# Routing weights loaded in one transfer behind the first input tile, and put in order by block transposes

## The chip, the cores and the metric

The kernel runs on one core of one Trainium2 chip. The metric is the device time of one execution in microseconds (us). A core has several engines with a queue of instructions each; those that matter here are VectorE (DVE), ScalarE (ACT) and SyncE (SP, which only issues transfers). All transfers between the main memory (HBM) and the on-chip memory (SBUF, 128 partitions) are carried by 16 DMA engines.

## The reference

```python
def setup_inputs():
    batch, seq, hidden, n_experts = 16, 1024, 512, 8
    k = 2
    ...

def reference(x, expert_indices, expert_weights):
    batch, seq, hidden = x.shape
    k = expert_indices.shape[-1]
    x_expanded = x[:, :, np.newaxis, :].repeat(k, axis=2)
    weights = expert_weights[..., np.newaxis]
    return (x_expanded * weights).astype(np.float32)
```

There are 16 x 1024 = 16,384 tokens. Each token's row of 512 float32 numbers is written out twice, once multiplied by each of its two weights. `expert_indices` is not used. The input x is 33.6 MB, the output 67.1 MB, the weights 128 KB.

## The kernel before

The 16,384 tokens are cut into 8 tiles of 2,048 tokens. In a tile, partition p holds 16 consecutive tokens (`TX = 16`): 16 rows of 512 numbers, 32 KB that lie in one piece in HBM. An x tile is therefore one transfer of 128 pieces of 32 KB (4 MB), an output tile one of 8 MB, 64 KB per partition in two halves of 8 tokens.

The weights of all tiles lie in one SBUF tile `w_tile` of 128 partitions x 256 numbers: 32 columns per token tile (16 tokens times 2). Partition p of tile g needs the 32 numbers of its own 16 tokens, a piece of 128 bytes in HBM. Line 57 loads them by 8 transfers on SP's queue, one for each token tile, each of 128 pieces of 128 bytes (16 KB). They are the first things in SP's queue.

`load(i)` (line 71) takes one of two x buffers and issues the transfer of x tile i on ScalarE's queue (line 78). Two tiles are loaded ahead; `load(i + 2)` stands at the end of the loop body for tile i.

The loop (line 83) runs over the 8 tiles. For each of the 16 tokens of a partition there are two multiplies of 128x512 numbers by a column of `w_tile`: VectorE makes copy 0 (`tensor_scalar`, line 99), ScalarE copy 1 (`mul`, line 93). Output tiles have two buffers. When the 16th token is done, SP issues the transfer of the output tile (line 109); the first tile alone is written in two halves, the first of them after 8 tokens. The output transfers stand in SP's queue behind the 8 weight transfers.

The waits between engines are put in by the framework, from what each instruction reads and writes. In the built program the first multiply of each engine waits for the first weight transfer and for the first x tile. Completions of transfers are counted on 8 semaphores taken in turn, so that some transfers wait for an earlier one that used the same semaphore: in this program the second x transfer waits for the second weight transfer, the eighth weight transfer for the first x tile, and the first output halves for the third and fifth weight transfer. The load of ScalarE's function table stands in ScalarE's queue behind the first two x transfers.

Of the kernel before, what the change touches and what calls it, by code (L numbers as in the profile page):

```python
# [1 line left out]

# [4 lines left out]


@with_exitstack
def kernel(  # L10
    ctx: ExitStack,
    tc: tile.TileContext,
    x: bass.AP,
    expert_indices: bass.AP,
    expert_weights: bass.AP,
    out: bass.AP,
):
    nc = tc.nc

    batch, seq, hidden = x.shape  # L20
    k = expert_weights.shape[-1]
    P = nc.NUM_PARTITIONS
    ntok = batch * seq
    assert ntok % P == 0
    A_TOTAL = ntok // P

    f32 = mybir.dt.float32
    row = k * hidden
    TX = 16
    TO = 16  # L30
    HALF = TO // 2
    PAD = 8


    groups = [[16], [16], [16], [16], [16], [16], [16], [16]]
    assert sum(sum(g) for g in groups) == A_TOTAL

    xf = x.rearrange("b s h -> (b s) h")
    of = out.rearrange("b s k h -> (b s) (k h)")
    wf = expert_weights.rearrange("b s k -> (b s) k")  # L40

    w_pool = ctx.enter_context(tc.tile_pool(name="w_pool", bufs=1))
    x_pool = ctx.enter_context(tc.tile_pool(name="x_pool", bufs=2))
    o_pool = ctx.enter_context(tc.tile_pool(name="o_pool", bufs=2))

    w_tile = w_pool.tile([P, A_TOTAL * k], f32)

    def rows(of_all, done, T):
        return of_all[done * P : (done + T) * P, :].rearrange(
            "(p a) n -> p (a n)", a=T  # L50
        )

    weights = []
    for group in groups:
        weights.append((sum(n for _, n in weights), sum(group)))
    for at, T in weights:
        nc.sync.dma_start(out=w_tile[:, at * k : (at + T) * k], in_=rows(wf, at, T))  # L57

    tiles = []
    done = 0  # L60
    for group in groups:
        T = sum(group)
        a0 = 0
        for n in group:
            tiles.append((done, T, a0, n))
            a0 += n
        done += T

    loaded = []

    def load(i):
        if i >= len(tiles):
            return
        done, T, a0, n = tiles[i]
        x_tile = x_pool.tile([P, TX * hidden], f32)
        cols = rows(xf, done, T)[:, a0 * hidden : (a0 + n) * hidden]
        for lo, hi in [(0, P)]:
            nc.scalar.dma_start(out=x_tile[lo:hi, : n * hidden], in_=cols[lo:hi, :])
        loaded.append(x_tile)

    for i in range(2):
        load(i)
    for i, (done, T, a0, n) in enumerate(tiles):
        x_tile = loaded[i]
        outr = rows(of, done, T)
        for t in range(n):
            if t % TO == 0:
                o_tile = o_pool.tile([P, 2, HALF * row + PAD], f32)
            for kk in range(k):
                c = (done + a0 + t) * k + kk  # L90
                h, o = t // HALF, t % HALF * row + kk * hidden
                if kk == 1:
                    nc.scalar.mul(  # L93
                        out=o_tile[:, h, o : o + hidden],
                        in_=x_tile[:, t * hidden : (t + 1) * hidden],
                        mul=w_tile[:, c : c + 1],
                    )
                    continue
                nc.vector.tensor_scalar(  # L99
                    out=o_tile[:, h, o : o + hidden],  # L100
                    in0=x_tile[:, t * hidden : (t + 1) * hidden],
                    scalar1=w_tile[:, c : c + 1],
                    scalar2=None,
                    op0=mybir.AluOpType.mult,
                )

            if t + 1 == TO or (i == 0 and t + 1 == HALF):
                halves = slice(h if i == 0 else 0, h + 1)
                nc.sync.dma_start(  # L109
                    out=outr.rearrange("p (b n) -> p b n", b=2)[:, halves, :],  # L110
                    in_=o_tile[:, halves, : HALF * row],
                )
        load(i + 2)

# [1 line left out]
_INS = ['x', 'expert_indices', 'expert_weights']  # L116
_OUTS = [((16, 1024, 2, 512), 'float32')]


# [23 lines left out]
```

## Time and profile before

| what | value |
|---|---|
| time, median of 4 runs | 240.77 us (239.89 to 241.2) |
| the profiled execution: its own time | 240.8 us |
| the profiled execution: its span | 239.0 us |
| busy: VectorE, ScalarE | 51.4 us (22%), 80.7 us (34%) |
| moved by the DMA engines | 100.81 MB in 4498 packets, mean 422 GB/s |
| queue q1 (SP's): packets, share of the 16 engines' span | 3344, 65.4% |
| queue q10 (ScalarE's): packets, share | 1152, 33.1% |
| the chain that ended last | DMA out_dram 51%, ACT 12%, DMA x_tile 10%, DMA w_tile 9% |
| issue to landing, median: weight transfer, x tile | 20.7 us, 23.9 us |

The span runs from the first to the last event of the profiled execution on the core; the device time has some 1.8 us more around it. Each queue's packets are what the DMA engines fetch from it: an x or output packet is 32 KB, a weight packet of line 57 128 bytes, and a few bytes more are semaphore updates. In the lists by line, the number behind the bar is busy time and the mean of one instruction, and behind the second bar stands how long the engine was idle before them and for whom it waited. DMA rates are booked where a packet starts.

### The profile page before, as it was taken

To read this page: it belongs to the slowest core of one execution; us is meant where nothing else is said; L and a number is where in the kernel's file an instruction comes from. 1 tells how busy PE (TensorE), PEld (TensorE's weight loads), DVE (VectorE), ACT (ScalarE), POOL (GpSimd) and SP (SyncE) were. 2 spreads that over 40 slices of the span, in tenths; PEclk is the share of its full clock that TensorE was granted. 3 is DMA by queue.
4 is the path that set the end of the run, shared out by engine and by line. 5 is a ranking of instruction groups with operands and counts; after the bars stand their busy time and mean duration, and the time that the engine had idled before them with its cause. 6 is when DMAs were issued, how large, how long until landed. Compare 5 with 4: busy or idle time off the path is not lost.

```text
span 239.0 us, 364 instructions
## 1 busy us (share of the span) xinstructions
DVE 51.4 (22%) x128; ACT 80.7 (34%) x129; POOL 0.2 (0%) x4
## 2 busy tenths in 40 slices
DVE  0073900019000036000064004600008205400000
ACT  0279950019500049200069004920008806900000
POOL 0000000000000000000000000000000000000000
DMA  7999999999999999999999999999999999999995
GB/s 266 440 440 367 439 439 439 433 428 433 417 433 422 429 428 440 433 439 439 439 439 439 417 439 411 439 411 422 439 433 433 439 439 439 433 433 439 433 433 219
DMA packets 4498, 100.81 MB, mean 422 GB/s; under 512 B 1424, under 2 KB 1424, under 8 KB 1424
## 3 DMA queue, kind: packets, MB, share of 16 engines
q1 hardware_dynamic: 3344, 67.24, 65.4%
q10 hardware_dynamic: 1152, 33.55, 33.1%
q14 instruction: 2, 0.02, 0.0%
HBM read 33.69 MB, written 67.11 MB: 422 GB/s over the span
## 4 chain that ended last, share of the span: by engine, by line
DMA 70%; ACT 12%; another core or an unknown queue 4%; SPq 1%; issue 0%; ACTq 0%
DMA out_dram<-o_tile 51%; ACT o_tile L93 12%; DMA x_tile<-in_x_dram 10%; DMA w_tile<-in_expert_weights_dram 9%; SPq L57 1%; ACTq L138 0%; ACTq L93 0%; SPq L109 0%
## 5 line engine op out<-in xcount | busy, mean ns | idle before, releaser
L93 ACT ACTIVATE o_tile<-x_tile,w_tile 128x512 f32<-128x512 f32 x128 | 79.5, 714 | 120.1 <-DMA out_dram<-o_tile 116.4
L99 DVE TENSOR_SCALAR o_tile<-x_tile,w_tile 128x512 f32<-128x512 f32 x128 | 51.4, 482 | 154.6 <-DMA out_dram<-o_tile 137.5
L93 ACT ACT_TABLE_LOAD x1 | 1.3, 1283 | 8.7 <-DMA w_tile<-in_expert_weights_dram 8.7
L127 POOL MEMSET const-bfloat16-1.0<- 128x1 bf16 x1 | 0.1, 102 | 0.0
L127 POOL MEMSET const-uint8-127<- 128x1 uint8 x1 | 0.1, 102 | 0.0
L127 POOL MEMSET const-float32-1.0<- 128x1 f32 x1 | 0.1, 100 | 0.0
L127 POOL MEMSET const-float32-0.0<- 128x1 f32 x1 | 0.1, 99 | 0.2 <-issue 0.2
## 6 DMA issues: line engine op xcount, KB each, us to landing
out_dram<-o_tile SPq DMA_DIRECT2D x7, 8192.0 KB, 48.4
x_tile<-in_x_dram ACTq DMA_DIRECT2D x8, 4096.0 KB, 23.9
out_dram<-o_tile SPq DMA_DIRECT2D x2, 4096.0 KB, 25.3
w_tile<-in_expert_weights_dram SPq DMA_DIRECT2D x8, 16.0 KB, 20.7
```

The source lines that it names most:

```text
L57: nc.sync.dma_start(out=w_tile[:, at * k : (at + T) * k], in_=rows(wf, at, T))
L93: nc.scalar.mul(out=o_tile[:, h, o : o + hidden], in_=x_tile[:, t * hidden : (t + 1) * hidden], mul=w_tile[:, c : c + 1],)
L99: nc.vector.tensor_scalar(out=o_tile[:, h, o : o + hidden], in0=x_tile[:, t * hidden : (t + 1) * hidden], scalar1=w_tile[:, c : c + 1], sc ...
L127: nc = _bacc.Bacc("TRN2", target_bir_lowering=False, num_devices=1)
```

## The change

The 8 weight transfers on SP go. Instead one transfer on ScalarE's queue, issued between the first and the second x tile, brings all 128 KB in HBM order into a new tile `w_in`: 128 pieces of 1 KB, partition p holding the numbers 256p to 256p + 255. Of these, 32 in a row are the weights of one partition of one token tile, but they lie on the wrong partition. VectorE puts them right in two steps of 32x32 block transposes: one of the whole tile (128x256, into `w_mid`), then 16 of 32x64, four for each source group of 32 partitions, which read `w_mid` in steps and write `w_tile`. One source group holds the weights of two token tiles, so `weights(src)` stands in front of every second tile of the loop. In the program as built, VectorE's order is: a memset, the 128x256 transpose, five of the 32x64 transposes, the 16 multiplies of tile 0, the other eleven transposes, and the rest of the multiplies.

A small activation on a tile of one column, set to zero by VectorE, is put into ScalarE's queue behind the transfers, so that the function table's load does not stand in front of a multiply. The multiplies, the two x and two output buffers, the transfers of x and of the output and their places in the loop are the same as before. In the built program, the second x transfer and the first three output transfers no longer wait for earlier transfers.

```diff
+    C = TX * k
+    B = 32
+    R = 8
...
-    for at, T in weights:
-        nc.sync.dma_start(out=w_tile[:, at * k : (at + T) * k], in_=rows(wf, at, T))
...
+    unused = w_pool.tile([P, 1], f32)
+    nc.vector.memset(unused, 0.0)
+
+    w_in = w_pool.tile([P, R * C], f32)
+    w_mid = w_pool.tile([P, R * C], f32)
+    w_tile = w_pool.tile([P, G * C], f32)
...
+        for n in pieces or [TX]:
+            cols = slice(at * hidden, (at + n) * hidden)
+            nc.scalar.dma_start(out=x_tiles[i][:, cols], in_=rows(xf, i)[:, cols])
+            if i == 0 and at == 0:
+                nc.scalar.dma_start(out=w_in, in_=wf.rearrange("(p n) -> p n", p=P))
+            at += n
 
-    for i in range(2):
-        load(i)
...
+    load([TX])
+    load()
+    nc.scalar.mul(out=unused, in_=unused, mul=unused)
...
+    nc.vector.transpose(out=w_mid, in_=w_in)
+    GQ = G // (P // B)
+
+    def weights(src):
+        for dst in range(P // B):
+            nc.vector.transpose(
+                out=w_tile[
+                    dst * B : (dst + 1) * B, src * GQ * C : (src + 1) * GQ * C
+                ],
+                in_=w_mid[src * B : (src + 1) * B, :].rearrange(
+                    "c (q g h j) -> c g h j q", q=R, g=GQ, h=P // B
+                )[:, :, dst],
+            )
+
+    for i in range(G):
+        if i % GQ == 0:
+            weights(i // GQ)
...
```

In the changed kernel the memset is line 56, the x transfers line 71, the weight transfer line 73, the small activation line 78, the first transpose line 85, the others line 90, the multiplies lines 111 (ScalarE) and 117 (VectorE), and the output transfers line 127.

## The prediction

> **What bounds the kernel now.** I read the page first, then the transfers and engines in stretches, then the order of time in the first 24 us, and last the transfers of 20 to 24 us in columns of 0.1 us.
>
> ```profile
> span 239.0 us, 364 instructions
> ...
> DMA  7999999999999999999999999999999999999995
> GB/s 266 440 440 367 439 439 439 433 428 433 417 433 422 429 428 440 433 439 439 439 439 439 417 439 411 439 411 422 439 433 433 439 439 439 433 433 439 433 433 219
> ...
> L93 ACT ACTIVATE o_tile<-x_tile,w_tile 128x512 f32<-128x512 f32 x128 | 79.5, 714 | 120.1 <-DMA out_dram<-o_tile 116.4
> L99 DVE TENSOR_SCALAR o_tile<-x_tile,w_tile 128x512 f32<-128x512 f32 x128 | 51.4, 482 | 154.6 <-DMA out_dram<-o_tile 137.5
> ```
>
> The 16 DMA engines are full in every slice but the first and the last, and ScalarE and VectorE mostly sit idle waiting for out_dram transfers. So the bytes bound the kernel, and an edit counts only by what it does to time in which the DMA engines carry no x or out bytes. Where is there such time? The next rows (stretch, then three engines' busy time, clock, DMA share, GB/s) answer.
>
> ```profile
> 0.00:24.00 24.00, 6.90 (x18) 11.69 (x18) 0.20 (x4) 1.00 0.94 377
> 24.00:232.00 208.00, 44.50 (x112) 69.05 (x112) 0.00 (x0) 1.00 1.00 433
> ```
>
> 433 GB/s is the running rate, from 24 us on without a hole; only the first 24 us are below it. x and out packets are 32 KB (x_tile: 33.55 MB in 1024 packets), so a round of one packet on each of 16 engines, 524,288 bytes, takes 524,288 / 433 GB/s = 1.21 us. There are 3072 / 16 = 192 rounds = 232.5 us. The other 6.5 us of the span are the start, one hole, and the end. The hole:
>
> ```profile
> 0.73 7.90 ACTq L78 DMA_DIRECT2D x_tile<-in_x_dram  x2
> 0.73 12.76 SPq L57 DMA_DIRECT2D w_tile<-in_expert_weights_dram  x8
> ...
> 13.17 9.94 ACT L93 ACTIVATE o_tile<-x_tile,w_tile 128x512 f32<-128x512 f32 x16 [3.23 <-DMA x_tile<-in_x_dram]
> ...
> 18.21 6.06 SPq L109 DMA_DIRECT2D out_dram<-o_tile  x2
> ```
>
> ```profile
> DMA  7700000999999900000000000024599999997000
> GB/s 329 329 0 0 0 0 0 329 987 658 1645 987 329 329 0 0 0 0 0 0 0 0 0 0 0 12 34 60 85 134 801 801 788 1086 1362 680 328 0 0 0
> DMA packets 884, 1.21 MB, mean 302 GB/s; under 512 B 850, under 2 KB 850, under 8 KB 850
> ```
>
> Column 0 of the second block is 20.0 us; bytes stand where their packet starts. The last round of the second input tile starts at 20.7 to 21.3 (mean, weighted by the columns, 21.03). The next big round, the first of the output, starts at 23.0 to 23.6 (mean 23.33): 2.30 us later, not 1.21. Yet its DMA was issued at 18.21. Between them, from 22.5, stand hundreds of 128-byte weight packets. SP's queue holds the weights of L57 ahead of the output of L109; while x flows, each engine takes about one weight packet per x packet, so most of the weights are still there when x ends, and the output waits behind them. That hole is 2.30 - 1.21 = 1.09 us.
>
> **The change part by part.**
>
> *The drain goes (T1).* SP issues no weights, so the first output half is alone in its queue. Gain 1.1 us if it is ready before x ends (below). Bounds: the stretch 22:24 started 0.62 MB of the 0.87 MB due at 433 GB/s, 0.25 MB or 0.6 us short; 20:25 shows 347 GB/s, 0.43 MB short or 1.0 us. So 0.6 to 1.1; I take 1.1, since whole rounds avoid cut-off packets.
>
> The Trainium skill, page "DMA: Bandwidth & Descriptors", section "Issuing engines are not separate DMA queues", speaks against this term: DMAs from several engines run on the same 16 engines, and another issuer saves issue time only. By that rule alone T1 would be 0 and the span about 238.6. The row differs: an output issued at 18.21 starts at 23.0, behind its own queue's packets.
>
> *Weight packets between x rounds (T2).* Rounds 2 to 16 start 3.95 (below) to 21.03, 14 intervals of 1.220 against 1.211 us: 0.1 us, gone.
>
> *The start (T3).* The transfers of 1.2 to 5.2 us show first x packets starting at 1.7 to 3.0 and the second round at 3.7 to 4.2, weighted mean 3.95. A first round at the running rate would have begun at 3.95 - 1.21 = 2.74; the first packet of any kind came at 1.7. So 1.0 us is lost, to read latency or to the 105 weight packets there. Low end: 336 weight packets had started by 22 us, so 1024 - 336 = 688 were left for the drain, 43 per engine in 1.09 us, 25 ns each; 105 / 16 = 6.6 of them are 0.16 us. None of it need be theirs: 0 to 1.0, no loss, as x leads its queue in both kernels. I take 0.5, between 0.16 and 1.0, because the x DMA issued beside the weights took 404 ns and all later ones 334: the two issues disturb each other.
>
> *The new weight DMA (T4).* 128 KB in 128 packets of 1 KB behind the first x tile in ScalarE's queue (L73): 8 per engine. By the drain's 25 ns: 0.2 us. By bytes at 32 KB in 1.21 us: 0.3. Twice that as the bad end: 0.6. I take 0.2, the small-packet row being nearer in size. Its issue (0.33 to 0.40 us, between the two x issues) costs nothing: the second x issue moves forward from 8.29 to about 1.5 us, and its bytes are not due until about 11.7. Without that cover each issue would cost its 0.4 us.
>
> *Transposes ahead of the first multiply.* The weights land after the first tile. That tile's multiply began at 13.17; minus T3 0.5, plus T4 0.2, the weights land at about 12.9. VectorE then runs one 128x256 and five 32x64 transposes (L85, L90), four of the five needed. The profile shows no transpose. From below, six at the MEMSET's 0.10 us: 0.6. From above, six at the 482 ns TENSOR_SCALAR of 512 elements: 2.9. By elements, 0.24 plus five at the floor of 0.10 is 0.74; with waits I take 1.0. First multiply 13.9; the eighth ACTIVATE ends 5.0 us later (13.17 to 18.21 before): output issue 18.9, data 1.0 later (issue 0.73, first packet 1.73): 19.9. x ends at 21.03 + 1.21 - 0.1 - 0.5 + 0.2 = 21.8. So 1.9 us of cover: cost 0. The second x tile then shares the engines from 19.9 to its end and lands near 24.6, later than 23.5. ACT, done with tile 0 at 23.8, waits, but 8.4 MB of output (19 us) keep the engines full meanwhile. The other 11 transposes stand on VectorE between tiles 0 and 1: at most 11 x 0.48 = 5.3 us, 20.3 to 25.6, then 6.4 us of multiplies to 32.0, still ahead of ACT's 34.5.
>
> A page's price for these: "Vector Engine (DVE) Microarchitecture Reference", section 3.8, gives the transpose array one element per cycle per lane; at the 0.96 GHz of "VectorE: DVE Perf Modes" 576 elements are an estimated 0.6 us, no row here shows it, and the sum would not move.
>
> *The rest.* The memset (L56) and the activation on it (L78) pull ACT_TABLE_LOAD, 1.28 us, from 8.66 to about 2 us; ACT idles to 13 us either way, so 0. Without that cover 1.4 us would delay the output, still under 1.9.
>
> **Sum.** -1.1 - 0.1 - 0.5 + 0.2 = -1.5 us: span 237.5, and the profiled execution 240.8 - 1.5 = 239.3; that execution stands 0.03 above the median 240.77, so 239.3 for the median too. The end (last packets, closing) is as before. Ends: best -1.1 - 0.1 - 1.0 + 0.2 = -2.0, worst -0.6 - 0.1 - 0 + 0.6 = -0.1.
>
> **Rivals.**
>
> *The ramp is read latency.* For: the second round starts on all engines within 0.5 us, whenever their first packet began (1.7 or 3.0), as if something common held them. Against: the longer x issue. T3 0, T4 0.3: -0.9, 239.9 us.
>
> *The hole only moves.* The first output's packets start late for another reason than the weights ahead of them, so T1 fails and only T2 and part of T3 remain: about -0.3, 240.5 us. Against: the column order of weights, then output.
>
> *Slower: the transposes empty the engines.* Place: VectorE between the landing of the weights and the first multiply, on which ScalarE and the first output wait. It decides once transposes take over 1.0 + 1.9 = 2.9 us; each further us is a us of idle DMA, and 0.5% slower needs 2.9 + 1.5 + 1.2 = 5.6 us, 0.93 us per instruction. At 1.0 us each: 6.0 - 2.9 = 3.1, minus 1.5: 242.4 us. For: their sources are read in strides of 32 elements, and no row prices that. Against: it is twice the longest VectorE row, on an eighth of its elements.
>
> **How the numbers follow.** Forecast 64%, latency ramp 20%, hole moves 4%, slower 12%. The likeliest gives 239.3. Half a per cent, about what a measurement of this kernel can tell from no change, is 1.2 us: the line is 239.57. Of the forecast 4 points fall inside it. Faster 60%, same 28%, slower 12%. The range takes the ends of the sum, 238.8 to 240.7, and, as single runs before spread over 1.3 us (239.89 to 241.2), 0.3 more below and 0.2 above: 238.5 to 240.9.
>
> **What will show it.** T1: no packets under 512 B, and output packets starting within 1.3 us of the last x round, or among x rounds. T3: the second x round near 3.45 instead of 3.95. T4: the first multiply at 13.5 to 14.5. Transposes: L85 and L90 on VectorE under 2.9 us ahead of it. A stretch near 22 us under 400 GB/s would say that the output came late; rates below 433 after 24 us would mean that the order of later transfers matters, which I left out.

## The result and the profile after

The changed kernel is slower, not faster: 241.36 us against 240.53 us (medians of 49 and 75 runs), ratio 1.0024 with a 95% interval of 1.0013 to 1.0035. Ratios leave out runs over 1.5% above the fastest of their kernel and need not equal the quotient of the medians. The profiled execution has a span of 239.4 us (239.0 before); the forecast was 237.5. The excess is small, a quarter of a per cent, but the forecast gain of 0.6% is not there at all.

The page of the changed kernel, the lines that answer to those of before:

```profile
span 239.4 us, 376 instructions
...
DMA  7999998999999999999999999999999999999993
GB/s 268 433 460 438 438 433 356 438 438 439 434 438 438 438 438 433 433 422 427 427 427 416 433 438 433 438 438 438 438 438 438 438 438 438 433 416 433 416 438 153
...
L111 ACT ACTIVATE o_tile<-x_tile,w_tile 128x512 f32<-128x512 f32 x128 | 79.3, 712 | 126.8 <-DMA out_dram<-o_tile 115.6
L117 DVE TENSOR_SCALAR o_tile<-x_tile,w_tile 128x512 f32<-128x512 f32 x128 | 51.4, 482 | 136.5 <-DMA out_dram<-o_tile 136.5
L90 DVE STREAM_TRANSPOSE w_tile<-w_mid 32x64 f32<-32x64 f32 x16 | 4.4, 277 | 0.3
L85 DVE STREAM_TRANSPOSE w_mid<-w_in 128x256 f32<-128x256 f32 x1 | 0.4, 447 | 12.4 <-DMA w_in<-in_expert_weights_dram 12.4
```

The fourth slice, 367 GB/s before, is 438: the hole near 22 us is gone. The seventh, 439 before, is 356: there x packets near 36 us are slow, of which more below. The last slice fell from 219 to 153. In order of time:

```profile
0.72 0.38 ACTq L71 DMA_DIRECT2D x_tile<-in_x_dram  x1
...
13.27 0.45 DVE L85 STREAM_TRANSPOSE w_mid<-w_in 128x256 f32<-128x256 f32 x1 [12.41 <-DMA w_in<-in_expert_weights_dram]
13.75 1.44 DVE L90 STREAM_TRANSPOSE w_tile<-w_mid 32x64 f32<-32x64 f32 x5
14.93 10.54 ACT L111 ACTIVATE o_tile<-x_tile,w_tile 128x512 f32<-128x512 f32 x17 [11.23 <-DVE w_tile L90]
...
19.97 15.34 SPq L127 DMA_DIRECT2D out_dram<-o_tile  x3
```

The first output is issued at 19.97, 1.8 us later than before. The transfers from 20 us in columns of 0.1 us show rounds at even distances: the last of x starts at 20.8 to 21.3, the first of the output at 22.0 to 22.5:

```profile
GB/s 983 328 0 0 0 0 0 0 655 328 983 1966 983 328 0 0 0 0 0 0 328 655 328 1311 1311 1311 0 0 0 0 0 0 328 655 328 983 1638 1311 0 0
DMA packets 68, 1.70 MB, mean 426 GB/s; under 512 B 16, under 2 KB 16, under 8 KB 16
```

In stretches, the first 24 us went from 377 to 399 GB/s, and the rate after them reads 431 (433 before; it is booked where a packet starts):

```profile
0.00:24.00 24.00, 10.52 (x31) 10.65 (x17) 0.20 (x4) 1.00 0.95 399
24.00:232.00 208.00, 45.83 (x115) 70.24 (x114) 0.00 (x0) 1.00 1.00 431
```

With each packet's bytes shared out evenly over its time, the changed kernel is 0.41 MB ahead at 24 us and still 0.31 MB, 0.7 us, at 232 us. What eats this is the very end. Transfers from 233 to 239 us in columns of 0.15 us, first the kernel before, then the changed one; one packet of 32 KB is 218 GB/s in such a column:

```profile
GB/s 437 218 218 0 218 437 1529 437 437 218 218 0 218 437 1529 437 437 0 437 0 0 0 655 218 0 0 0 0 0 0 0 0 0 0 0 0 0 0 0 0
```

```profile
GB/s 0 218 1092 874 1311 0 0 0 0 0 1311 874 1311 0 0 0 0 0 219 0 0 0 0 0 0 0 218 0 0 0 0 0 0 0 0 0 0 0 0 0
```

Before, the last packets start from 235.1 to 236.6 us, several at a time. After, 16 packets start from 234.5 to 234.92 us (the second group), and then single ones at 235.72 and 236.93: 15 engines are done, and one still has two packets to move, alone. The kernel ends when the slowest engine ends: the span closes 1.19 us (before) and 1.26 us (after) behind the end of the last packet.

The packet records name no engine, but as each engine moves one packet after the other, packets can be strung together into 16 chains (start to the end just before); in four of the five profiles below each chain then has 192 packets of 32 KB, 3072 / 16. From them, worked out from the records: the start of the 17th packet of 32 KB (the first of the output) on the median engine, the end of the last packet on the median engine and on the latest, and how far the latest is behind the median there.

```
kernel          first output issued  17th packet  median ends  latest ends  latest behind
before                18.21             23.36        236.58       237.81        1.23
before_copy           18.24             23.33        236.95       238.27        1.32
before_copy2          18.26             23.57        236.59       237.19        0.60
after                 19.97             22.40        235.94       238.14        2.20
after_copy            20.00             22.31        236.01       238.17        2.16
```

The median engine gains 0.96 us at the hole and still has 0.64 of it at its end. The latest engine falls 0.97 us further behind and takes it all back: -0.64 + 0.97 = +0.33, the close is 0.07 longer, and the span grew by 0.4.

### The profile page after: what moved, and what is told of

It is laid out like the page before. It is cut to its first block, busy times and chain, and to the rows that moved or that the text cites. A ratio compares the mean times of both kernels' runs of the same rounds, so it can differ in the third digit from the quotient of the medians.

```text
span 239.4 us, 376 instructions
## 1 busy us (share of the span) xinstructions
DVE 56.3 (24%) x146; ACT 80.9 (34%) x130; POOL 0.2 (0%) x4
## 4 chain that ended last, share of the span: by engine, by line
DMA 66%; ACT 16%; another core or an unknown queue 4%; issue 1%; DVE 1%; ACTq 0%
DMA out_dram<-o_tile 50%; ACT o_tile L111 16%; DMA x_tile<-in_x_dram 10%; DMA w_in<-in_expert_weights_dram 5%; DVE w_tile L90 0%; ACTq L156 0%; DVE w_mid L85 0%; ACTq L71 0%; ACTq L111 0%
## 5 line engine op out<-in xcount | busy, mean ns | idle before, releaser
L117 DVE TENSOR_SCALAR o_tile<-x_tile,w_tile 128x512 f32<-128x512 f32 x128 | 51.4, 482 | 136.5 <-DMA out_dram<-o_tile 136.5
L90 DVE STREAM_TRANSPOSE w_tile<-w_mid 32x64 f32<-32x64 f32 x16 | 4.4, 277 | 0.3
```

The source lines that it names most:

```text
L90: nc.vector.transpose(out=w_tile[dst * B : (dst + 1) * B, src * GQ * C : (src + 1) * GQ * C], in_=w_mid[src * B : (src + 1) * B, :].rearrange(
L117: nc.vector.tensor_scalar(out=o_tile[:, h, o : o + hidden], in0=in_, scalar1=w_tile[:, c : c + 1], scalar2=None, op0=mybir.AluOpType.mult,)
```

## The experiments

All are timed beside the kernel before on the same chip; ratios are to it. In the table, "17th" and "behind" are worked out as above, from the one profiled execution of each run, whose own time stands behind them.

```
run             first output  17th    behind  profiled us  median us   ratio (95%)
after_copy         20.00      22.31    2.16     241.23      241.52    1.0031 (1.0008-1.0054)
before_copy        18.24      23.33    1.32     241.24      240.90    1.0007 (0.9979-1.0034)
before_copy2       18.26      23.57    0.60     240.16      240.16    one run
after_w_sp         19.39      22.79    1.27     241.28      242.60    1.0051 (1.0022-1.0080)
before_w1_act      20.07      22.58    2.90     242.43      243.59    1.0120 (1.0078-1.0162)
after_plus_w8      20.49      26.16    0.43     242.77      243.10    1.0089 (1.0057-1.0121)
after_no_tr        18.51      23.26    2.44     241.99      241.01    1.0014 (0.9989-1.0040)
no_tr_delay        20.58      22.36    4.40     244.55      244.38    1.0158 (1.0141-1.0175)
before_delay       20.50      22.73    3.75     243.33      243.46    1.0128 (1.0102-1.0155)
before_w_pool      19.94      22.55    0.99     240.85      243.21    1.0084 (1.0049-1.0119)
w_pool_early       18.58      23.26    0.98     241.21      240.97    1.0007 (0.9980-1.0033)
nudge1             20.14      22.30    2.57     241.68      241.93    1.0054 (1.0026-1.0082)
nudge2             20.04      22.27    2.18     241.16      242.00    1.0068 (1.0041-1.0094)
oneq_after         20.21      22.39    2.99     242.44      242.25    1.0061 (1.0034-1.0088)
oneq_w_act         19.91      25.70    2.64     244.69      244.59    1.0146 (1.0108-1.0184)
```

Where the profiled execution is far from the median (before_w_pool and after_w_sp are well under it), "behind" need not be that of a typical run.

**Is the late engine there again?** Both kernels unchanged, for more profiles.

> The changed kernel unchanged, for a second profile. Theory S (straggler): the hole near 22 us is closed here too, 15 of the 16 DMA engines finish some 0.7 us earlier than before, but one engine finishes about 2 us behind the others and sets the end; time 241.1 to 241.6 us, and the stretch from 235.5 us on again shows single packets (about 27 GB/s, one engine) after the others are done. Theory N (accident): the late engine was a chance of the one profile; this profile ends with all engines within 1 us and a span near 237.5 us, and the excess over before comes from elsewhere (running rate below 433 GB/s after 24 us).

> The kernel before unchanged, for a second profile. Theory S: the hole at 22.5 to 23 us (1.1 us) is there again, and the engines' ends lie within about 1.7 us, so that the span is 238.5 to 239.2 us. Theory N: the ends are spread as widely as in the changed kernel (2 us or more) and the span moves with it.

> The kernel before unchanged, for a third profile of its ends: hole of about 1 us at 22.5 us again, 17th round at 23.3 us, latest engine 0.5 to 1.3 us behind the mean, against 1.9 to 2.1 in the changed kernel's two profiles.

It is: 2.16 us behind in the second profile of the changed kernel, against 0.6 to 1.3 in three of the kernel before. Theory S holds, N falls, but in after_copy three engines are late (1.62, 1.81 and 2.16 us behind), not one. The bound set for the span of before_copy was missed by little (239.5).

**Was the hole the weights' drain?** First the parts of the change by themselves.

```diff
-                nc.scalar.dma_start(out=w_in, in_=wf.rearrange("(p n) -> p n", p=P))
+                nc.sync.dma_start(out=w_in, in_=wf.rearrange("(p n) -> p n", p=P))
```

> The changed kernel with its one weight transfer (1 KB runs) at the head of SP's queue instead of behind the first x tile on ScalarE's. If the place in ScalarE's queue costs engine time (0.3 to 0.5 us per engine between the first and the second x tile), this is faster than the changed kernel by that much, about 240.9 us, since 8 packets per engine flow beside the 8 x packets and nothing is left to drain. If the straggler sets the end (theory S), the average engine finishes earlier but the time moves only if the late engine does: 239.5 or 241.3, not between.

Not faster: 1.0051, an interval that overlaps the changed kernel's. In its profile, of a run 1.3 us under the median, the late engine is gone (1.27), but the 17th packet starts at 22.79. The output was issued at 19.39, earlier than in the changed kernel.

```diff
+    nc.scalar.dma_start(
+        out=w_tile.rearrange("p (g n) -> p g n", g=8),
+        in_=wf.rearrange("(g p a) k -> p g (a k)", g=8, p=P),
+    )
```

> The kernel before with all weights in one transfer of 1024 runs of 128 bytes behind the first x tile in ScalarE's queue, straight into tile order: no transposes, nothing ahead of the output on SP. 64 packets per engine between the x tiles at the 16 to 25 ns of the drain cost 1.0 to 1.6 us per engine where before lost 1.2, so the average engine ends as before or 0.4 later: 240.5 to 241.0 us. If the place alone were what made the changed kernel slow, with its order of later transfers, this one ends like it, near 241.3 with one late engine; if the transposes were, it ends at 240.5.

Slower than every theory said, 1.0120. 128-byte runs cost less at that place than expected, 0.6 us between the first and the second x tile on the median engine instead of 1.0 to 1.6, and the hole closes; but two x packets at 36 us take 1.4 and 1.6 us too long, and the latest engine ends 2.90 us behind.

```diff
-    nc.vector.transpose(out=w_mid, in_=w_in)
...
-            weights(i // GQ)
```

> The changed kernel without its 17 transposes (the multiplies take the weights as they were loaded, so the output differs from the reference). The first multiply begins some 1.7 us earlier, at about 13.2 us. Rival P: if the transposes' delay of the first output cost time, 239.5 to 240.0 us. Theory S: the DMA engines have no hole near 22 us with or without them, so the average engine ends where the changed kernel's does (236.1 to 236.4) and the time is whatever its latest engine makes of it, 239.2 or 241.3.

This run turned the question round. No weights stand in SP's queue and the output is issued at 18.51, and the hole is back, 23.26. Transfers of 20 to 24 us in columns of 0.1 us:

```profile
GB/s 983 0 655 0 0 0 0 0 0 328 655 1311 1638 655 328 328 0 0 0 0 0 0 0 0 0 0 0 0 983 655 328 328 655 655 655 655 328 0 0 0
```

Theory S's sentence that there is no hole with or without transposes is wrong; and the earlier output does not help the time (1.0014, as before and not told apart from the changed kernel; the profiled run, a slower one of its runs, has a latest engine 2.44 us behind). So three idle multiplies were put where the transposes had been, and the same three into the kernel before:

```diff
+        if i == 0:
+            for _ in range(3):
+                nc.vector.tensor_scalar(
+                    out=o_tile[:, 0, hidden : 2 * hidden],
...
```

> The changed kernel without transposes, and with three idle multiplies on VectorE in their place, so that the first output is issued near 20.2 us instead of 18.5 (output differs from the reference, as the weights are not put in order). Theory D (the hole near 22 us comes from the output setting in while x packets are still in flight, and closes when its packets arrive as x runs out): no hole, the 17th round of 32 KB packets starts at 22.3 to 22.5 us on the median engine, as in the changed kernel, against 23.26 without the delay. Rival W (the hole is the weights' drain on SP's queue, and what the kernel without transposes showed was something else): 23.2 us again.

> The kernel before with the same three idle multiplies: the first output is issued near 20.2 us instead of 18.21, with the eight weight transfers ahead of it in SP's queue as before. Theory D: the hole shrinks from 1.1 to 0.3 to 0.6 us, what is left being the weight packets (688 x 13 ns / 16 = 0.56 us); the 17th round starts at 22.6 to 22.9 us, and the time is 240 us or under unless an engine falls behind later. Rival W: the hole stays at 1.1 us or grows, 17th round at 23.36 or later.

Theory D holds in both for the hole: 22.36 and 22.73, with the weights still ahead of the output in the second. Its time for before_delay, 240 us or under unless an engine falls behind, was not met: both kernels are over 1% slower, with the latest engine 4.40 and 3.75 us behind. In before_delay the drain of the weights is what is left of the hole, from 21.9 us on:

```profile
GB/s 328 329 0 329 0 0 1 328 987 659 986 1316 329 329 0 329 0 0 0 10 23 62 94 454 483 1114 762 1068 1352 26 342 338 0 0 0 0 0 0 328 983
```

The size of the hole by itself is the step from the 16th to the 17th packet on the median engine, less the usual 1.21 us:

```
                                    output issued early            output issued late
weights ahead of it in its queue    before        2.31: 1.10       before_delay  1.66: 0.45
none ahead of it                    after_no_tr   2.05: 0.84       no_tr_delay   1.23: 0.02
```

So the early output is worth 0.65 to 0.82 us of the hole, and the weights 0.26 to 0.43. The split is rough, as it rests on one profile each and the two copies of before give 2.27 and 2.64. Rival W needed the weights off SP's queue in the kernel before itself:

```diff
-        nc.sync.dma_start(out=w_tile[:, at * k : (at + T) * k], in_=rows(wf, at, T))
+        nc.gpsimd.dma_start(out=w_tile[:, at * k : (at + T) * k], in_=rows(wf, at, T))
```

> The kernel before with the eight weight transfers issued by GpSimd, on a queue of their own; nothing stands ahead of the output on SP, which is issued at 18.2 us as before. Theory D (the hole comes from the output setting in while x packets are in flight): the hole stays, the 17th round starts at 23.1 to 23.4 us on the median engine. Rival W (the hole is the wait behind the weights): output packets start near 19.5 us and there is no hole, 17th round at 22.3 us or earlier.

17th packet at 22.55, but this decides nothing, because the function table's load had come to stand behind the first x tile and the output was issued at 19.94. With the small activation of the changed kernel added ahead:

```diff
+    nc.scalar.mul(out=unused, in_=unused, mul=unused)
```

> The kernel before with the weights on GpSimd's queue, and with the small activation of the changed kernel ahead, so that ScalarE's function table is loaded early and the first output is issued at 18.2 to 18.5 us (without the activation it was 19.94, too late to tell the two apart). Theory D (the hole comes from an output that sets in while x packets are in flight): the hole is back, the last x packets are stretched to 1.6 us and more and the 17th round starts at 23.0 to 23.4 us on the median engine. Rival W (the hole is the wait behind the weights on SP's queue): no hole, 17th round at 22.5 us or earlier.

Theory D said this: 23.26. (From GpSimd the weights moved in 128 packets of 1 KB on a queue of their own.) The issue, and the transfers of 20 to 24 us in columns of 0.1 us:

```profile
18.58 5.25 SPq L112 DMA_DIRECT2D out_dram<-o_tile  x2
```

```profile
GB/s 1341 666 1034 655 0 0 0 0 0 0 655 328 1311 655 655 1639 0 0 0 0 0 0 0 0 0 0 0 0 0 20 993 338 2038 666 348 338 666 0 0 0
DMA packets 96, 1.43 MB, mean 359 GB/s; under 512 B 28, under 2 KB 53, under 8 KB 53
```

The last x round starts at 21.0 to 21.5, the output at 23.0 to 23.6, and from 21.6 to 22.8 us no packet of x, output or weights starts: there is no drain. For comparison the same columns of no_tr_delay, whose output was issued two microseconds later and starts one earlier (22.0 to 22.6, the third group):

```profile
GB/s 983 328 328 0 0 0 0 0 655 328 1638 983 983 328 328 0 0 0 0 0 328 328 983 1639 1311 328 328 0 0 0 0 0 0 0 0 983 1311 328 328 0
```

Rival W is out as the whole cause; its share is the 0.3 to 0.4 us above. Leaving out the two runs below whose second x transfer was issued late, an output issued at 18.2 to 18.6, while the second x tile still has two or three rounds to go, has its first packet at 23.3 to 23.6 on the median engine; issued at 19.9 to 20.6, at 22.3 to 22.7; at 19.39, at 22.79. The last x packets ahead of it are stretched to between 1.5 and 2.3 us in before, after_no_tr and w_pool_early; in no_tr_delay and before_delay they take 1.21. Why the engines do not take turns there, as they do from 29 us on, is not shown.

**What holds one engine up?** In the changed kernel's profile one output packet, started at 134.97 us, takes 2.43 us, twice the usual 1.21; in after_copy three take 2.16 to 2.43 at the same time. It is the moment at which x sets in again (issue 131.00, first packets some 4 us later) after a stretch of output alone. By the chains, this one packet puts its engine 1.22 us further behind. The same engine had lost 0.6 us at 58 to 60 us, and it loses 0.2 more at 145: that is most of its 2.2 us. Transfers of 133 to 137 us in columns of 0.1 us, one packet 328 GB/s:

```profile
GB/s 1311 1311 655 0 0 0 328 0 0 0 0 1638 983 983 983 328 0 0 0 328 0 0 0 1638 983 655 1311 328 0 0 0 0 0 0 0 1638 983 655 1311 328
```

The round from 134.1 has 15 packets and a straggler at 134.9; the next two rounds, from 135.3 and from 136.5, have 15 packets each and no straggler in between. The sixteenth engine misses a turn. Idle ACTIVATEs between the fifth tile's multiplies and that load (one in nudge1, two in nudge2) move the moment:

```diff
+        if i == 4:
+            for _ in range(1):
+                nc.scalar.mul(out=scratch, in_=o_tile[:, 1, o : o + hidden], mul=x_tile[:, :1])
         load()
```

> The changed kernel with one ACTIVATE more, on a tile that nothing reads, between the last multiply of the fifth tile and the load of the seventh input tile: that load's issue moves from 131.0 to about 131.8 us, and ScalarE has 15 us to spare there. Theory R (an engine is held up by up to a packet when a queue sets in, and which engine by how much hangs on the moment): the 2 us of the late engine at 135 us change, to 0 to 1 us or to another engine; time anywhere from 239.3 to 242 us, but not the changed kernel's 241.1 to 241.6. Rival A (the lateness belongs to one DMA engine or to the addresses): no change, 241.1 to 241.6 with one engine 2 us late.

> The same with two such ACTIVATEs, so that the load's issue is at about 132.4 us. Theory R: again another spread of the engines' ends, different from that of one ACTIVATE and of none. Rival A: 241.1 to 241.6 us with one engine 2 us late.

The issue moves from 131.00 to 131.92 and 132.44, and the doubled packets from 134.97 to 135.9, 136.6 and 136.8 (three engines) and to 135.7 and 136.2 (two). Transfers of 134 to 138 us in nudge2, in the same columns: 15 packets from 134.0 and a straggler at 134.8, again 15 from 135.2 and a straggler at 136.2, and only 14 in the round from 136.4. The turns are missed one round later.

```profile
GB/s 655 983 983 1638 328 328 0 0 328 0 0 0 655 983 983 1311 655 328 0 0 0 0 328 0 655 983 983 1311 655 0 0 0 0 0 0 0 655 983 983 1311
```

So the hold-up moves with the load's issue and is not tied to one moment. But the latest engine is still 2.57 and 2.18 us behind and the kernels are no faster, which theory R had left open and did not foretell.

Next, x in packets of 16 KB, so that x, taken in turn with 32 KB of output, does not run dry in between:

```diff
-        x_tiles.append(x_pool.tile([P, TX * hidden], f32, name="x_tile"))
+        x_tiles.append(x_pool.tile([P, 2, HALF * hidden + PAD], f32, name="x_tile"))
...
+                out=x_tiles[i][:, :, : HALF * hidden],
+                in_=rows(xf, i).rearrange("p (b n) -> p b n", b=2),
```

> The changed kernel with a pad of 8 numbers in the middle of each input row in SBUF, so that x moves in 2048 packets of 16 KB instead of 1024 of 32 KB. Taken in turn with output packets of 32 KB, x then gets a third of the engines' time while both queues have work, as much as it needs, and its queue does not run dry while output is left. Theory R (a form of S: an engine is held up, by up to a whole packet of 1.2 us, where x sets in again after a stretch of output alone, at 28 and 135 us): such stretches go, the 16 engines end within 0.7 us of each other and the time is 239.0 to 239.9 us. If the hold-ups have nothing to do with x setting in again: 241 us or more, with one or more engines 2 us late.

> The kernel before with the same pad, x in packets of 16 KB. Theory R: its hold-ups go too, but the hole of 1.1 us stays, so this takes 0.5 to 1.0 us longer than the changed kernel with the pad: 239.9 to 240.6 us. If the hole is worth nothing even so, the two are equal within 0.3 us.

The engines end within 0.2 us of each other in both profiles, as theory R said, and after 25 us no packet of after_x16k takes over 0.8 us longer than usual (two in before_x16k do, 1.2 and 1.6 us). But this doesn't show it, for the time is not the forecast 239.0 to 239.9 and 239.9 to 240.6 but worse, 245.06 us (1.0131, interval 1.0075 to 1.0187) and 245.86 us (1.0203, 1.0158 to 1.0249): the last x tile is now late, the engines run empty while its multiplies run, and a common stop of that kind levels them. Three stretches of after_x16k:

```profile
215.00:220.00 5.00, 1.92 (x5) 5.00 (x9) 0.00 (x0) 1.00 0.62 269
220.00:225.00 5.00, 0.00 (x0) 0.23 (x1) 0.00 (x0) 1.00 0.74 315
225.00:230.00 5.00, 0.00 (x0) 0.00 (x0) 0.00 (x0) 1.00 1.04 446
```

Only the last two tiles in 32 KB packets again:

> The changed kernel with x of the first six tiles in packets of 16 KB and of the last two in packets of 32 KB, so that the last input is not late as it was with 16 KB throughout (hole of 2.8 us at 220 us). Theory R: x does not set in again before the sixth tile has landed, engines end within 1 us of each other, and the time is 239.0 to 240.2 us. Rival A: an engine 2 us late, 241 us or more.

The hole at the end is gone (433 GB/s from 215 to 225 us), but 245.86 us, 1.0219 (1.0181 to 1.0257), and the engines end 2.2 us apart. Against the expectation, and its single runs spread from 242.35 (the profiled one) to 247.17, so this settles nothing.

**All transfers in one queue**, where no queue can set in beside another:

```diff
-            nc.scalar.dma_start(out=x_tiles[i][:, cols], in_=rows(xf, i)[:, cols])
+            nc.sync.dma_start(out=x_tiles[i][:, cols], in_=rows(xf, i)[:, cols])
```

> The changed kernel with x and the weights issued on SP's queue too, so that all transfers of x and out stand in one queue and no queue sets in beside another. Theory R (engines are held up where a queue sets in beside a busy one): no hold-ups after 20 us, all 16 engines end within 0.5 us of each other at 236.0 to 236.6 us, time 238.8 to 239.8 us, faster than both kernels. Rival A (one engine is late for a reason of its own): one or more engines 1 to 2 us late as in the changed kernel, 241 us or more. If reads and writes one after the other are slower than mixed, the rate after 24 us falls below 433 GB/s and the time rises with all engines together.

> The kernel before with the queues changed: x and out together on SP, the eight weight transfers of 128-byte runs alone on ScalarE's queue, no transposes. Theory R with D: the weights take turns with the x and out packets, one for one, and are never waited for by an output; no hole, no hold-ups, time within 0.5 us of the same kernel with 1 KB runs and transposes, 238.8 to 240 us. Rival W (128-byte runs cost the engines time wherever they stand): 0.6 to 1.1 us longer than that kernel.

Theory R is refuted in its strict form: 1.0061, and one engine is 3 us late here too (2.99). Packets are held where output and x follow each other in the one queue too (0.4 to 0.9 us on all 16 engines at 50.3 us). Rival W's ground, the price of 128-byte runs, was not met cleanly: in oneq_w_act the second x transfer waited for the first on the same semaphore and was issued only at 13.05 us (17th packet 25.70). (The kernel before has a wait of that kind too: by the trace its second x transfer, issued at 8.29, waits for the first weight transfer, and its first two output transfers for the second and the fourth, one earlier each than said at the top.) Such a wait, for a weight transfer, spoils the last run as well, which puts the old transfers back beside the new one:

```diff
+        nc.sync.dma_start(
+            out=w_old[:, g * C : (g + 1) * C],
...
```

> The changed kernel, which also loads the weights in the old way: the eight transfers of 128-byte runs stand at the head of SP's queue again, into a tile that nothing reads. Theory S (the end is set by the DMA engine that loses most, and how much it loses hangs on how the 16 engines stand in time to each other): the hole of about 1 us is back and the average engine ends 1.0 to 1.3 us later than in the changed kernel, at about 237.3, but the time is not that much more: 240.2 to 241.4 us, as the late engine's 2 us are not simply added. Rival P (the change's own parts, the transfer behind the first tile and the transposes, cost what was lost): all costs add, 242.3 to 242.7 us.

243.10 us, above what S expected and above rival P's band (242.3 to 242.7) as well, and for a reason that neither had: the second x transfer was issued only at 13.55 us, and the median engine loses 2.6 us more there than in the changed kernel. Its engines are even (0.43 behind) after the common stop.

No version beat the kernel before.

## Why the prediction was wrong

- **T1, the hole (forecast -1.1).** The size was right: from the 16th to the 17th packet the median engine takes 1.26 us instead of 2.31, so -1.05. The reason was right in its lesser part. "The output waits behind them" (the weights) is worth 0.26 to 0.43 us; after_no_tr and w_pool_early have no weights ahead, and most of the hole. Seeing 128-byte packets in the hole, I took what filled it for its cause. What closed the rest was the transposes, by making the first output late, a step that I had priced at 0 behind 1.9 us of cover. So that T1 came out whole was luck: without the transposes' time most of the hole stays (after_no_tr), as "the hole only moves" said, whose reason was the better one though its number was not.
- **T2, between the rounds (-0.1)** is too small to be seen apart.
- **T3, the start (-0.5)** was mis-sized: the second round starts at 3.84 on the mean instead of 3.96, -0.1. The longer issue on which I leaned (404 ns) is no sign of a disturbance: with no other issue beside it, it takes 0.38 us in the changed kernel. The low end, and T4, used 25 ns for a weight packet, but the records say 13; the drain did not fill the hole. The rival "the ramp is read latency" was right in that the second round starts there with and without weights; that it is read latency is not shown.
- **T4, the weight transfer (+0.2).** Its packets took 46 ns each, 8 per engine 0.37 us; the 5th to the 10th packet on the median engine take 6.40 us instead of 6.11, so +0.3. With T1 to T3 that makes the 0.96 us by which the 17th packet starts earlier, against the forecast 1.5.
- **The transposes** took 1.66 us (13.27 to 14.93) against my 1.0, inside my 0.6 to 2.9; 277 ns for 64 elements per partition. The first output was issued at 19.97 instead of 18.9, and its first packet came 2.0 us behind the issue (22.0), not 1.0: it did not join the x packets, as I had it, but followed them. The slower rival, that they empty the engines, did not happen, though the kernel is slower.
- **Left out**: x packets at 35.7 us stretched by 0.4 us on all 16 engines in both profiles of the changed kernel, where the output queue had just run dry; +0.4. So the median engine gains 0.64 of the 1.5.
- **The step that failed**: "The end (last packets, closing) is as before." I treated 16 engines as one and summed a mean engine. The latest engine went from 1.23 us behind (0.6 to 1.3 in three profiles) to 2.20 (2.16 in the second profile), and these 0.97 us cost more than the 0.64 that the rest gave. Most of its 2.2 us can be read off the chains: 1.22 in a doubled packet where x sets in again at 131 us, moved by the nudges, 0.6 at 58 to 60 us, 0.2 at 145.
- **What stays open**: why doubled packets hit some engines and not the others; in after, after_copy and nudge2 the latest engine is the one that was already the furthest behind before its doubled packet, by 0.5 to 0.6 us. The kernel before has such a packet too: in before_copy one of 2.59 us at 144.94 makes its latest engine. Also open is whether kernels with the hole closed are hit more, and why: the latest engine is 2.2 to 4.4 us behind in after, after_copy, no_tr_delay, before_delay, before_w1_act, oneq_after and the nudges, but 0.99 in before_w_pool; with the hole it is 0.6 to 1.3 behind in four profiles, but 2.44 in after_no_tr. No run took the late engine away and left all else as it was, so that the changed kernel would then be the faster one is not shown.

## What to carry to other kernels

Where transfers bound a kernel as here, the end is that of the slowest DMA engine: look at the last slice and the packets that start after the others have stopped before summing an average engine. A gain of under 1% early in such a kernel can be lost to what one engine loses later, so it is read from the end, not from the stretch that was mended. What stands in a hole isn't thereby its cause; take it away alone, and keep the issue times of all else, before it is priced.

## What was not expected of the hardware

- An output issued 1.5 to 2 us later had its first packet 0.8 to 1 us earlier (18.5 to 18.6 gives 23.26 in after_no_tr and w_pool_early; 20.0 to 20.6 gives 22.3 to 22.4 in after, after_copy and no_tr_delay).
- Some packets of 32 KB took up to twice their time (2.16 to 2.43 us against 1.21), on one to three engines, at the moment when a second queue began.
- With x in 16 KB packets the profiles look even, yet single runs differ by up to 7 us (242.0 to 248.81 in after_x16k), while those of the changed kernel's copy differ by 1.8.
- A fetch of instructions (8 KB, one packet, twice in each profile; at 58.0 and 62.7 us in the changed kernel, 81.4 and 92.5 before) takes 0.31 us and goes with an x or out packet of 0.35 us over its time; at 58.0 us in the changed kernel's profile that is the 0.6 us of the engine which is late at the end, by the chains worked out above.
